# TensorE in program order, and transposes one slot later in three attentions

## The chip, the cores and the metric

The kernel runs on one core of a Trainium2 chip. A core has TensorE (PE: matmuls and transposes, into PSUM), VectorE (DVE), ScalarE (ACT), GpSimd (POOL) and SyncE (SP, whose queue issues the DMAs). Each engine works through its own list of instructions and waits where a semaphore says that an input or a buffer isn't there. The metric is the device time of one execution in microseconds, as the median of several runs.

## The reference, cut to what matters

Two transformer layers are computed one after the other in float32. The first, on 16 meta and 512 other tokens, has three branches on one projection: retention, differential attention (`probs0 - lam * probs1`, 8 heads) and a short convolution, then gates, an output product and a feed-forward part. The second, on 512 tokens and 256 context tokens, has a feed-forward part, projections, a neighbourhood attention (8 heads), a latent attention (8 heads, `softmax(q k^T) v`), gates and a second feed-forward part. Both layers use RMS norms:

```python
def rms_norm(x, w):
    xf = x.astype(jnp.float32)
    y = xf * lax.rsqrt(jnp.mean(xf * xf, axis=-1, keepdims=True) + EPS)
    return (y * w.astype(jnp.float32)).astype(x.dtype)
```

## The kernel before, in words

Every large product is computed with operands split in a high and a low part, three matmuls for one. Activations lie transposed in SBUF, features on partitions and tokens along the row. `Emitter._gemm` (its matmul is L231) takes 128 output columns at a time. For each it loops over the k tiles, and for each k tile over the three matmuls, into a PSUM buffer: `psg` or `pss`, two of each. Weights come by DMA as `raw`; ScalarE makes the high part `whi` (L132), VectorE or GpSimd the low part `wlo` (L136), in units of 512 columns with four buffers of each (`nhl=4`). The buffers of a unit come free when its matmuls have run.

The attentions are generators ("background"). While products are emitted, `tick` adds the model time of each matmul, `w / 2.4 + 3` ns, to a credit. Whenever it reaches the pace (3000 ns in retention, 900 in the differential, 750 in the neighbourhood and 700 in the latent attention), the generator is run to its next `yield`. At a `drain` it is run to its end. Each of the three attentions has 32 steps (head and block of 128 queries) in stages: `s0` scores on TensorE and the row maximum, `s1` the exponential and the scaling, `s2` transposes of the probabilities into PSUM (`pst`, two buffers) and their split into high and low parts, `s3` the product with v, and in the differential attention `s4` and `s5`, the norm and the transposes of its result. In slot t stage k handles step t - k, so a step's transposes come two slots behind its scores. The neighbourhood attention has at each head a matmul with `J` (L1511) that makes the bias table `TB`.

Norms run as a chain: sums of squares, a matmul with ones (`sums`, L330), some twenty tiny VectorE instructions, diagonal matrices, and a matmul (`spread`, L349) that lays the factor over all partitions. `em.after` puts the sums and the spread later in the emission by a given model time. `start2` emits the whole first chain at once, ahead of the first product.

What sets the order on the engines: the program is written out in full and then ordered by a scheduler. It plays the program through with a model of the durations. On each engine it picks, among the instructions that it takes as ready, the one of highest priority, which is the one emitted first (the weight splits are moved 30 places forward). So an instruction that isn't ready in the model is passed by others that were emitted after it. The lists so made are fixed when the kernel runs.

The names and lines of the steps: L231 weight products; L277 to L279 `mm3`, the scores in retention (h = q parts `qh`, `ql`) and in the latent attention (`mQ`, `mK`); L330 and L349 `sums` and `spread`; L806 transposes of the differential attention, whose input is `de`; `dvs`, that stage's split of the transposed v.

Of the kernel before, what the change touches and what calls it, by code (L numbers as in the profile page):

```python
# [6 lines left out]
F32 = mybir.dt.float32  # L7
F32R = mybir.dt.float32r
# [36 lines left out]
class Emitter:  # L45
# [19 lines left out]

    def open_streams(s, const, psum, nraw=3, nhl=4):
        s.sp, s.psum, s.nraw, s.nhl = const, psum, nraw, nhl


    def gemm(s, unit, cols, rhs, segs, evac, kt=KT):  # L70
# [140 lines left out]
    def _gemm(s, it):  # L211
        nc = s.nc
        jobs = it.segs if it.kind == "gemm" else it.chunks
        src = it.rhs if it.kind == "gemm" else it.lhs
        step = 512 // it.cols
        for si, job in enumerate(jobs):
            c0, w = job
            xh, xl = src(si)
            tag = s.rot[s.rot_i % len(s.rot)]
            s.rot_i += 1  # L220
            ps = s.psum.tile([128, 512 if tag == "g" else 1024], F32, name="ps" + tag, tag=tag, bufs=2)
            out = ps[0:it.cols, 0:w] if it.kind == "gemm" else ps[0:w, 0:it.cols]
            for k in range(it.kt):
                j = it.first + k // step
                s._step(j)
                cs = slice(it.cols * (k % step), it.cols * (k % step + 1))
                wh, wl = (t[:, cs] for t in s.hl[j])
                for m, (a, b) in enumerate(((wh, xh), (wh, xl), (wl, xh))):
                    b = b[:, k, c0:c0 + w]
                    l, r = (a, b) if it.kind == "gemm" else (b, a)  # L230
                    nc.tensor.matmul(out, l, r, start=(k == 0 and m == 0), stop=(k == it.kt - 1 and m == 2))  # L231
                    s._step()
                    s.tick(max(w if it.kind == "gemm" else it.cols, 64) / 2.4 + 3)
                if si == len(jobs) - 1 and (k == it.kt - 1 or k % step == step - 1):
                    s.hl.pop(j)
                    s._plan_split()
            s.late.append(lambda si=si, out=out: it.evac(si, out))
            s.flush_late(s.lag)


class Pools:
# [16 lines left out]

def emit(tc, d, out, dbg=None, stop=None):
    nc = tc.nc  # L260
    V, A, G, T, SP = nc.vector, nc.scalar, nc.gpsimd, nc.tensor, nc.sync
    pools = Pools(tc)
    em = Emitter(tc)
    psum = pools.open("psum", space=PSUM)
# [416 lines left out]
    DF = {}  # L681

    def d_evac(h, what):
        def f(si, ps):
            p, R1 = S["dp"], S["R1"]
            segs = TAIL if what == "q" else HALF
            c0, n = segs[si]
            r = R1[:, c0:c0 + n]
            A_, B_ = slice(0, 64), slice(64, 128)
            em.require(lambda: h < 2 or ("dS", h - 2) in GEMMED)  # L690
            if what == "q":
                v = p.tile([128, 512], F32, name="dev", tag="dev", bufs=2)
                DF[h, "q"] = [p.tile([128, 512], F32R, name=f"q{m}", tag=f"q{m}", bufs=2) for m in range(2)]
                hi = p.tile([128, 528], F32R, name="dhi", tag="dhi")
                lo = p.tile([128, 528], F32R, name="dlo", tag="dlo")
                V.tensor_mul(v, ps, r)
                act(hi[:, 0:512], v)
                sub_lo(G, lo[:, 0:512], v, hi[:, 0:512])
                for m, X in enumerate((A_, B_)):
                    spill(DF[h, "q"][m][A_], hi[X, 0:512])  # L700
                    spill(DF[h, "q"][m][B_], lo[X, 0:512])
            elif what == "k":
                if si == 0:
                    DF[h, "k"] = [[p.tile([128, 528], F32R, name=f"k{e}{m}", tag=f"k{e}{m}", bufs=2) for e in "hl"]
                                  for m in range(2)]
                    DF["k"] = [p.tile([128, 528], F32R, name="d" + e, tag="d" + e) for e in ("hi", "lo")]
                hi, lo = DF["k"]
                v = p.tile([128, 512], F32, name="dev", tag="dev", bufs=2)
                V.tensor_mul(v[:, 0:n], ps, r)
                cs = slice(c0, c0 + n)  # L710
                act(hi[:, cs], v[:, 0:n])
                sub_lo(G, lo[:, cs], v[:, 0:n], hi[:, cs])
                if si == 1:
                    for m, X in enumerate((A_, B_)):
                        for k, src in zip(DF[h, "k"][m], (hi, lo)):
                            for Y in (A_, B_):
                                spill(k[Y], src[X])
            else:
                if si == 0:
                    DF[h, "v"] = p.tile([128, 528], F32, name="dvt", tag="dvt", bufs=2)  # L720
                V.tensor_mul(DF[h, "v"][:, c0:c0 + n], ps, r)
            if si == len(segs) - 1:
                GEMMED.add(("d", h, what))
        return f
# [3 lines left out]
    def diff_bg():  # L728
# [3 lines left out]
        def s0(i):  # L732
# [3 lines left out]
                t = L["T", h] = p.tile([128, 528], F32, name="dT", tag="dT")  # L736
                V.tensor_scalar_mul(t, S["dbase"], -8.0 * 2.0 ** (-(h + 1)))
            tb = L["T", h]
            e = L["e", i] = p.tile([128, 2, 528], F32, name="de", tag="de", bufs=3)
            sm = L["sm", i] = p.tile([128, 8], F32, name="dsm", tag="dsm", bufs=3)  # L740
            ps, src = None, []
            for m in range(2):
# [109 lines left out]
            hilo(S["dfh"][:, h, :], S["dfl"][:, h, :], ps, w08)  # L852

        stages = (s0, s1, s2, s3, s4, s5)
        order = (5, 4, 1, 3, 0, 2)
        stage_runs = lambda k, i: k == 3 or i % 4 == 3
        for slot in range(32 + len(stages) - 1):
            if slot < 32:
                while ("d", slot // 4, "v") not in GEMMED:
                    yield False  # L860
            for k in order:
                if 0 <= slot - k < 32:
                    sub = stages[k](slot - k)
                    if sub is not None:
                        yield from sub
                    if k < 3 or stage_runs(k, slot - k):
                        yield

    em.low_parts(G, G)
# [601 lines left out]
    def stack(n, what, first, t0, u):  # L1471

        p = S["na"]
        N = 512 if what == "q" else 768
        cs = slice(t0, t0 + u.shape[-1])
        if first:
            NA["hl"] = [p.tile([128, 768], F32R, name="n" + c, tag="n" + c) for c in ("hi", "lo")]
        hi, lo = NA["hl"]
        act(hi[:, cs], u)
        sub_lo(G, lo[:, cs], u, hi[:, cs])  # L1480
        if t0:
            return
        if what == "q":
            NA[n, "q"] = [p.tile([128, 512], F32R, name=f"nq{e}", tag=f"nq{e}", bufs=2) for e in range(2)]
        else:
            NA[n, "k"] = [[p.tile([128, 768], F32R, name=f"nk{c}{e}", tag=f"nk{c}{e}", bufs=2) for c in "hl"]
                          for e in range(2)]
        for e, X in enumerate((A_, B_)):
            if what == "q":
                spill(NA[n, "q"][e][A_], hi[X, 0:N])  # L1490
                spill(NA[n, "q"][e][B_], lo[X, 0:N])
            else:
                for k, src in zip(NA[n, "k"][e], (hi, lo)):
                    for Y in (A_, B_):
                        spill(k[Y], src[X])
# [3 lines left out]
    def na_bg():  # L1499
# [3 lines left out]
        def s0(i):  # L1503
# [16 lines left out]
            wl = 128 * (hi - lo)  # L1520
            w = wl + 256
            q = NA[n, "q"][e][:, 128 * j:128 * j + 128]
            P_ = L["P", i] = p.tile([128, 640], F32, name="nP", tag="nP", bufs=3)
            sm = L["sm", i] = p.tile([128, 4], F32, name="nsm", tag="nsm", bufs=4)
            ps = pss()
            for a, c0, cw in ((512 - wl, 128 * lo, wl), (512, 512, 256)):
                for m, k in enumerate(NA[n, "k"][e]):
# [64 lines left out]
                GEMMED.add(("na", n))  # L1592

        stages = (s0, s1, s2, s3)
        order = (1, 3, 0, 2)
        stage_runs = lambda k, i: i % 4 == 3
        for slot in range(32 + len(stages) - 1):
            if slot < 32:
                while ("na", slot // 8, "v") not in GEMMED:
                    yield False  # L1600
                if slot % 8 == 0:
                    vprep(slot // 8)
            for k in order:
                if 0 <= slot - k < 32:
                    sub = stages[k](slot - k)
                    if sub is not None:
                        yield from sub
                    if k < 3 or stage_runs(k, slot - k):
                        yield

    def fold(o, p, e, oh, ol, w=512):
# [66 lines left out]
    def ml_bg():  # L1678
# [3 lines left out]
        def s0(i):  # L1682
# [4 lines left out]
                ml_load(h + 1)  # L1687
            Q, K = ML["Q", e], ML["K", e]
            qs = slice(128 * j, 128 * j + 128)
            P_ = L["P", i] = p.tile([128, 2, 384], F32, name="mP", tag="mP", bufs=3)  # L1690
            sm = L["sm", i] = p.tile([128, 4], F32, name="msm", tag="msm", bufs=4)
            ps = pss()
            L["S", i] = ps.rearrange("p (a k) -> p a k", a=2)[:, :, 0:384]
# [39 lines left out]
            fold(o, p, e, S["OMH"][:, n, q0:q0 + 256], S["OML"][:, n, q0:q0 + 256], 256)  # L1733

        stages = (s0, s1, s2, s3)
        order = (1, 3, 0, 2)
        stage_runs = lambda k, i: i % 2 == 1
        for slot in range(32 + len(stages) - 1):
            for k in order:
                if 0 <= slot - k < 32:  # L1740
                    sub = stages[k](slot - k)
                    if sub is not None:
                        yield from sub
                    if k < 3 or stage_runs(k, slot - k):
                        yield

    def ona_evac(n):
# [228 lines left out]
```

## Time and profile before

| what | value |
|---|---|
| median of three runs | 2831.26 us (2831.24 to 2832.66) |
| the profiled execution | 2835.28 us |
| its span, first to last instruction | 2833.3 us |
| mean granted TensorE clock | 0.984 |
| TensorE matmuls, weight loads | 97%, 85% of the span |
| VectorE, ScalarE, GpSimd | 57%, 39%, 30% |

The profiled execution is one execution; the rows and sums below are of its span, and the 2 us around it belong to its time. TensorE's ends are modelled, so a busy TensorE need not be at its peak.

### The profile page before, as it was taken

To read this page: it belongs to the slowest core of one execution; us is meant where nothing else is said; L and a number is where in the kernel's file an instruction comes from. 1 tells how busy PE (TensorE), PEld (TensorE's weight loads), DVE (VectorE), ACT (ScalarE), POOL (GpSimd) and SP (SyncE) were. 2 spreads that over 40 slices of the span, in tenths; PEclk is the share of its full clock that TensorE was granted. 3 is DMA by queue.
4 is the path that set the end of the run, shared out by engine and by line. 5 is a ranking of instruction groups with operands and counts; after the bars stand their busy time and mean duration, and the time that the engine had idled before them with its cause. 6 is when DMAs were issued, how large, how long until landed. Compare 5 with 4: busy or idle time off the path is not lost.

```text
span 2833.3 us, 42915 instructions
## 1 busy us (share of the span) xinstructions
PE 2736.0 (97%) x16308; PEld 2405.3 (85%) x16308; DVE 1620.0 (57%) x3318; ACT 1092.5 (39%) x2201; POOL 849.9 (30%) x710
## 2 busy tenths in 40 slices
PE   9999999999999889899999999979999999899997
PEld 8889988888878667788888888868889998899897
DVE  6554422377757999555223233496576876834346
ACT  4333322445534222243222122354455665633233
POOL 0223323433324233242111112442333224323224
PEclk9999999999999999999999999989999999999998
DMA  4222222443225658332121221334643424332324
GB/s 136 73 68 91 96 97 93 129 125 102 83 93 191 205 195 295 114 108 68 53 75 60 61 66 60 93 117 156 179 102 103 133 62 162 133 97 90 93 94 127
DMA packets 115998, 316.95 MB, mean 112 GB/s; under 512 B 21680, under 2 KB 35376, under 8 KB 115536
## 3 DMA queue, kind: packets, MB, share of 16 engines
q1 hardware_dynamic: 115792, 314.21, 35.5%
q8 instruction: 129, 2.11, 0.3%
q14 instruction: 77, 0.63, 0.1%
HBM read 279.09 MB, written 13.83 MB: 103 GB/s over the span
## 4 chain that ended last, share of the span: by engine, by line
PE 80%; DVE 14%; issue 3%; ACT 2%; DMA 0%; POOL 0%; POOLq 0%; DVEq 0%; SPq 0%; ACTq 0%
PE psg L231 49%; PE pss L231 22%; DVE wlo L136 2%; DVE wa L995 2%; DVE wx L995 1%; PE pss L277 1%; PE pst L827 1%; PE pss L278 1%; PE pss L279 1%; PE pst L1731 1%; PE pst L1717 1%; PE pss L1528 1%; PE pst L824 0%; DVE ut L1045 0%; DVE mg L1224 0%
## 5 line engine op out<-in xcount | busy, mean ns | idle before, releaser
L136 POOL TENSOR_TENSOR wlo<-raw,whi 128x512 fp32r<-128x512 f32 (+1 forms) x442 | 580.1, 1313 | 1568.4 <-ACT whi L132 1527.4
L132 ACT ACTIVATE whi<-raw 128x512 fp32r<-128x512 f32 (+1 forms) x844 | 522.7, 622 | 927.8 <-PE psg L231 588.8
L136 DVE TENSOR_TENSOR wlo<-raw,whi 128x512 fp32r<-128x512 f32 (+1 forms) x402 | 314.0, 782 | 452.6 <-ACT whi L132 451.9
L231 PE MATMUL psg<-xl,whi 128*128 128x264 f32 (+2 forms) x1104 | 362.7, 329 | 0.9 <-DVE xl L403 0.9
L231 PE MATMUL psg<-xh,whi 128*128 128x264 f32 (+2 forms) x1104 | 361.4, 328 | 1.7 <-ACT whi L132 1.2
L231 PE MATMUL psg<-xh,wlo 128*128 128x264 f32 (+2 forms) x1104 | 361.7, 328 | 0.0
L231 PE MATMUL psg<-XH,whi 128*128 128x256 f32 (+3 forms) x984 | 308.2, 313 | 1.8 <-DVE ft L1136 1.0
L231 PE MATMUL psg<-XH,wlo 128*128 128x256 f32 (+3 forms) x984 | 308.2, 313 | 0.0
L231 PE MATMUL psg<-XL,whi 128*128 128x256 f32 (+3 forms) x984 | 307.8, 313 | 0.0
L231 PEld LDWEIGHTS psg<-xh,whi 128*128 128x128 f32 x1104 | 209.0, 189 | 18.8 <-ACT whi L132 1.4
L231 PEld LDWEIGHTS psg<-xl,whi 128*128 128x128 f32 x1104 | 209.1, 189 | 18.5 <-DVE xl L403 1.5
L231 PEld LDWEIGHTS psg<-xh,wlo 128*128 128x128 f32 x1104 | 209.2, 190 | 17.0 <-DVE wlo L136 0.2
L231 PE MATMUL pss<-XL,whi 128*128 128x256 f32 (+2 forms) x600 | 191.3, 320 | 6.1 <-DVE XL L1208 6.1
L231 PEld LDWEIGHTS psg<-XH,whi 128*128 128x128 f32 (+1 forms) x984 | 185.4, 188 | 11.5 <-issue 2.4
L231 PEld LDWEIGHTS psg<-XH,wlo 128*128 128x128 f32 (+1 forms) x984 | 185.8, 189 | 10.5 <-issue 0.2
L231 PEld LDWEIGHTS psg<-XL,whi 128*128 128x128 f32 (+1 forms) x984 | 185.8, 189 | 9.3
L231 PE MATMUL pss<-XH,wlo 128*128 128x256 f32 (+2 forms) x600 | 191.4, 319 | 1.2 <-DVE wlo L136 1.2
L231 PE MATMUL pss<-XH,whi 128*128 128x256 f32 (+2 forms) x600 | 190.9, 319 | 0.5 <-DVE fs L1128 0.5
L231 PEld LDWEIGHTS pss<-XL,whi 128*128 128x128 f32 x600 | 114.9, 192 | 14.3 <-DVE XL L1208 7.3
L231 PEld LDWEIGHTS pss<-XH,wlo 128*128 128x128 f32 x600 | 115.4, 192 | 10.1 <-DVE wlo L136 1.6
L231 PEld LDWEIGHTS pss<-XH,whi 128*128 128x128 f32 x600 | 114.9, 192 | 7.5 <-DVE fs L1128 0.7
L231 PE MATMUL pss<-hh,wlo 128*128 128x256 f32 (+1 forms) x296 | 101.8, 344 | 7.5 <-DVE wlo L136 7.5
(558 smaller groups left out, 6444.6 us busy)
## 6 DMA issues: line engine op xcount, KB each, us to landing
raw<-w SPq DMA_DIRECT2D x142, 512.0 KB, 3.3
raw<-wi SPq DMA_DIRECT2D x96, 512.0 KB, 3.3
wa<-wa SPq DMA_DIRECT2D x72, 512.0 KB, 4.2
raw<-wq SPq DMA_DIRECT2D x38, 512.0 KB, 3.5
raw<-wu SPq DMA_DIRECT2D x32, 512.0 KB, 4.2
raw<-wd SPq DMA_DIRECT2D x32, 512.0 KB, 4.1
raw<-wb SPq DMA_DIRECT2D x24, 512.0 KB, 3.2
raw<-wo SPq DMA_DIRECT2D x24, 512.0 KB, 4.0
```

The source lines that it names most:

```text
L132: s.nc.scalar.activation(h, raw, AF.Copy)
L136: eng.tensor_sub(l, raw, h.bitcast(F32))
L231: nc.tensor.matmul(out, l, r, start=(k == 0 and m == 0), stop=(k == it.kt - 1 and m == 2))
L277: T.matmul(o, wh, xh, start=first, stop=False)
L278: T.matmul(o, wh, xl, start=False, stop=False)
L279: T.matmul(o, wl, xh, start=False, stop=last)
L827: T.matmul(o, x[:, c, :], vs[:, c, :], start=False, stop=c == b and m == 1)
L995: V.tensor_tensor_reduce(o, w, sb[:, s_, :], 1.0, 0.0, ALU.mult, ALU.add, S["modc"][:, s_, j:j + 1])
L1528: T.matmul(ps[:, a:a + cw], q, k[:, c0:c0 + cw], start=m == 0, stop=m == 1)
L1717: T.transpose(ps[:, 128 * c:128 * c + 128], P_[:, 128 * (c0 + c):128 * (c0 + c) + 128], ident)
L1731: T.matmul(o[:, 0:256], v[:, c, :], x[:, c, :], start=c == 0 and m == 0, stop=c == 5 and m == 1)
```

## The change

Every matmul and transpose is made through a wrapper, which ties it to the instruction that TensorE got before it. The scheduler may not move one past another any more; the other engines are ordered as before. In the three attentions stage `s2` and the stages behind it come one slot later, so the transposes stand three slots behind the scores. Tiles that live a slot longer get one buffer more (`de`, `nP`, `nsm`, `mP`), and the high and low parts of q and k that are copied by DMA get two buffers instead of one (`dhi`, `dlo`, `nhi`, `nlo`).

```diff
     def open_streams(s, const, psum, nraw=3, nhl=4):
         s.sp, s.psum, s.nraw, s.nhl = const, psum, nraw, nhl
+        s.pe = InOrder(s.tc, s.nc.tensor)
...
-                    nc.tensor.matmul(out, l, r, start=(k == 0 and m == 0), stop=(k == it.kt - 1 and m == 2))
+                    s.pe.matmul(out, l, r, start=(k == 0 and m == 0), stop=(k == it.kt - 1 and m == 2))
...
+class InOrder:
+
+
+    def __init__(s, tc, eng):
+        s.tc, s.eng = tc, eng
+
+    def matmul(s, *a, **kw):
+        s.tc.keep_in_program_order(s.eng.matmul(*a, **kw))
+
+    def transpose(s, *a, **kw):
+        s.tc.keep_in_program_order(s.eng.transpose(*a, **kw))
+
+
...
-    V, A, G, T, SP = nc.vector, nc.scalar, nc.gpsimd, nc.tensor, nc.sync
+    V, A, G, T, SP = nc.vector, nc.scalar, nc.gpsimd, InOrder(tc, nc.tensor), nc.sync
...
-                hi = p.tile([128, 528], F32R, name="dhi", tag="dhi")
-                lo = p.tile([128, 528], F32R, name="dlo", tag="dlo")
+                hi = p.tile([128, 528], F32R, name="dhi", tag="dhi", bufs=2)
+                lo = p.tile([128, 528], F32R, name="dlo", tag="dlo", bufs=2)
...
-            e = L["e", i] = p.tile([128, 2, 528], F32, name="de", tag="de", bufs=3)
+            e = L["e", i] = p.tile([128, 2, 528], F32, name="de", tag="de", bufs=4)
...
         stages = (s0, s1, s2, s3, s4, s5)
+        lags = (0, 1, 3, 4, 5, 6)
         order = (5, 4, 1, 3, 0, 2)
         stage_runs = lambda k, i: k == 3 or i % 4 == 3
-        for slot in range(32 + len(stages) - 1):
+        for slot in range(32 + lags[-1]):
...
             for k in order:
-                if 0 <= slot - k < 32:
-                    sub = stages[k](slot - k)
+                i = slot - lags[k]
+                if 0 <= i < 32:
+                    sub = stages[k](i)
                     if sub is not None:
                         yield from sub
-                    if k < 3 or stage_runs(k, slot - k):
+                    if k < 3 or stage_runs(k, i):
                         yield
...
-            NA["hl"] = [p.tile([128, 768], F32R, name="n" + c, tag="n" + c) for c in ("hi", "lo")]
+            NA["hl"] = [p.tile([128, 768], F32R, name="n" + c, tag="n" + c, bufs=2) for c in ("hi", "lo")]
...
-            P_ = L["P", i] = p.tile([128, 640], F32, name="nP", tag="nP", bufs=3)
-            sm = L["sm", i] = p.tile([128, 4], F32, name="nsm", tag="nsm", bufs=4)
+            P_ = L["P", i] = p.tile([128, 640], F32, name="nP", tag="nP", bufs=4)
+            sm = L["sm", i] = p.tile([128, 4], F32, name="nsm", tag="nsm", bufs=5)
...
-            P_ = L["P", i] = p.tile([128, 2, 384], F32, name="mP", tag="mP", bufs=3)
+            P_ = L["P", i] = p.tile([128, 2, 384], F32, name="mP", tag="mP", bufs=4)
```

The loops of the neighbourhood and the latent attention get `lags = (0, 1, 3, 4)` in the same way.

## Rows read from the trace of the kernel before

**Rows 1.** The page's engine table: busy us, share of the span, instructions.
```profile
PE 2736.0 (97%) x16308; PEld 2405.3 (85%) x16308; DVE 1620.0 (57%) x3318; ACT 1092.5 (39%) x2201; POOL 849.9 (30%) x710
```

**Rows 2.** Stretches: length, then busy us of each engine, granted clock, DMA share, GB/s.
```profile
530.00:792.00 262.00, 252.89 (x1604) 219.98 (x1603) 186.05 (x561) 133.75 (x376) 96.95 (x80) 0.99 0.37 107
...
1300.00:1400.00 100.00, 100.00 (x566) 87.24 (x565) 40.02 (x68) 28.04 (x49) 18.31 (x18) 1.00 0.19 59
...
2020.00:2330.00 310.00, 308.31 (x2159) 287.75 (x2158) 234.22 (x610) 177.41 (x398) 87.05 (x70) 1.00 0.41 106
```

**Rows 3.** TensorE's waits from 530 to 792: total us, times, longest.
```profile
PE pst L806 <- DVE dvs L274: 4.8, 4, 2.0
```

**Rows 4.** Timeline of the start (start, us), and L349 there.
```profile
7.89 0.39 PE L231 MATMUL psg<-xh,whi 128*128 128x264 f32 x1 [1.22 <-ACT whi L132]
...
19.03 0.69 DVE L136 TENSOR_TENSOR wlo<-raw,whi 128x512 fp32r<-128x512 f32 x1
...
19.27 1.08 PE L330 MATMUL pst<-ones,acc 128*128 128x1 f32 x10
...
L349 PE MATMUL pst<-acc,ones x4: 258/436/697, 25.9 to 27.1; 128*128 128x512 f32 x2, 16*128 16x16 f32 x2
```

**Rows 5.** Stretches of L231 alone: length, matmuls' and loads' busy us (count), clock, DMA.
```profile
7.89:25.90 18.01, 16.01 (x95) 13.27 (x95) 1.00 0.71 238
...
71.90:74.40 2.50, 2.12 (x17) 1.88 (x15) 1.00 0.00 0
...
87.70:88.90 1.20, 1.20 (x5) 0.81 (x5) 1.00 0.00 0
...
532.80:536.10 3.30, 3.21 (x13) 2.16 (x13) 1.00 0.90 206
...
786.80:790.70 3.90, 2.72 (x12) 1.87 (x10) 1.00 0.13 33
...
1290.60:1293.40 2.80, 2.80 (x13) 2.07 (x11) 1.00 0.01 3
...
1862.00:1882.80 20.80, 17.17 (x124) 16.16 (x124) 0.89 0.29 92
...
1953.60:1960.10 6.50, 6.25 (x30) 4.85 (x28) 1.00 0.81 295
...
2031.00:2043.00 12.00, 9.79 (x54) 7.76 (x52) 1.00 0.54 128
...
2170.00:2181.60 11.60, 9.42 (x74) 8.97 (x73) 1.00 0.67 171
...
2457.60:2463.60 6.00, 5.85 (x50) 5.64 (x48) 1.00 0.51 173
```

**Rows 6.** Timeline in retention, second head: VectorE's `ql` and the scores.
```profile
73.34 0.98 DVE L274 TENSOR_TENSOR ql<-ev,qh 128x512 fp32r<-128x512 f32 x1 [0.70 <-ACT qh L271]
...
74.39 0.50 PE L278 MATMUL pss<-ql,kh 128*128 128x512 f32 x1
```

**Rows 7.** A stretch of the neighbourhood attention, columns as in rows 2.
```profile
2040.00:2055.00 15.00, 15.00 (x96) 13.20 (x94) 13.34 (x38) 9.45 (x22) 5.71 (x5) 1.00 0.56 117
```

**Rows 8.** The latent attention: an issue, `mQ` from issue to landing, the first scores.
```profile
2176.19 0.58 SPq L1674 DMA_DIRECT2D mQ<-qr_d  x1
...
DMA to landing us min/median/max: 5.4/6.8/8.0
...
2189.86 0.34 PE L277 MATMUL pss<-mK,mQ 96*128 96x384 f32 x1
```

**Rows 9.** A wait of a transpose, and two stretches as in rows 2.
```profile
578.85 0.33 PE L806 MATMUL pst<-ident,de 128*128 128x128 f32 x1 [1.99 <-DVE dvs L274]
...
580.00:583.00 3.00, 3.00 (x16) 3.00 (x15) 2.75 (x12) 0.30 (x1) 0.00 (x0) 0.50 0.79 181
...
938.00:948.00 10.00, 5.08 (x12) 3.17 (x11) 9.83 (x15) 1.26 (x2) 2.55 (x2) 0.50 0.52 170
```

More of the change, by code (lines that the diff above doesn't have):

```diff
@@ L705, in f @@
                                   for m in range(2)]
-                    DF["k"] = [p.tile([128, 528], F32R, name="d" + e, tag="d" + e) for e in ("hi", "lo")]
+                    DF["k"] = [p.tile([128, 528], F32R, name="d" + e, tag="d" + e, bufs=2) for e in ("hi", "lo")]
                 hi, lo = DF["k"]
@@ L1594, in na_bg @@
         stages = (s0, s1, s2, s3)
+        lags = (0, 1, 3, 4)
         order = (1, 3, 0, 2)
         stage_runs = lambda k, i: i % 4 == 3
-        for slot in range(32 + len(stages) - 1):
+        for slot in range(32 + lags[-1]):
             if slot < 32:
@@ L1603, in na_bg @@
             for k in order:
-                if 0 <= slot - k < 32:
-                    sub = stages[k](slot - k)
+                i = slot - lags[k]
+                if 0 <= i < 32:
+                    sub = stages[k](i)
                     if sub is not None:
                         yield from sub
-                    if k < 3 or stage_runs(k, slot - k):
+                    if k < 3 or stage_runs(k, i):
                         yield
@@ L1735, in ml_bg @@
         stages = (s0, s1, s2, s3)
+        lags = (0, 1, 3, 4)
         order = (1, 3, 0, 2)
         stage_runs = lambda k, i: i % 2 == 1
-        for slot in range(32 + len(stages) - 1):
+        for slot in range(32 + lags[-1]):
             for k in order:
-                if 0 <= slot - k < 32:
-                    sub = stages[k](slot - k)
+                i = slot - lags[k]
+                if 0 <= i < 32:
+                    sub = stages[k](i)
                     if sub is not None:
                         yield from sub
-                    if k < 3 or stage_runs(k, slot - k):
+                    if k < 3 or stage_runs(k, i):
                         yield
```

## The prediction

> **What bounds the kernel now.** The page's engine table comes first: TensorE is busy 2736.0 us of the 2833.3 us span, 97%, and its weight loads 2405.3 us [rows 1]. All of TensorE's idle time together is therefore 97 us, and in a stretch such as 1300 to 1400 us there is none: 100.00 us busy at the full granted clock [rows 2]. Second, the waits: the largest group in the attentions is a transpose's, 4.8 us in four waits [rows 3]. So the change can give back little, and the question is what it takes away. Now the scheduler picks, among matmuls and transposes whose inputs it takes as ready, the one emitted first; one that isn't ready is passed by. Afterwards nothing is passed. I therefore followed the code's emission order and looked in the timeline for matmuls that run ahead of an instruction emitted before them. Each such place is a wait that is filled today. Its price is the busy time of the line that fills it, L231, from where TensorE would first stand before the waiting instruction to where that one's inputs are there [rows 5]. TensorE has no slack behind most of these places, so a filled wait that becomes an empty one moves the end.
>
> **The change part by part.**
>
> *Start.* `start2` emits the sums (L330) and the spread of R1 (L349) ahead of every weight product. In the rows the first weight product starts at 7.89 us, the sums at 19.27, the spread at 25.9 [rows 4]. Between, L231 ran 95 matmuls, 16.0 us [rows 5]. In program order none of them may run before the spread. The chain in front of it shortens a little: four weight splits run on VectorE between sums and spread, some 0.68 us each, the first at 19.03 [rows 4]. Their buffers come free only when products run, so they fall out of the chain: 2.7 us. Cost 16.0 - 2.7 = 13.3 us; bounds 10 and 16.
>
> *Retention.* The scores are emitted right behind the q product, whose evacuation is not done. The scores' second matmul runs at 74.39, when `ql` of 73.34 + 0.98 us is there [rows 6]; L231 filled 2.1 us. The transposes of v wait likewise for a PSUM buffer, 1.2 us [rows 5]. Each comes once for each of four heads: 4 x 2.1 + 4 x 1.2 = 13.2 us. Bounds 8 (if the evacuation comes sooner when it has VectorE alone) and 16.
>
> *Differential attention.* 3.2 us at the first scores, which wait for spilled q and k, and 2.7 us at the last transposes, which wait for the norm [rows 5]: 5.9 us. What of the idle time goes? The transposes L806 wait on `dvs` [rows 3], which is the evacuation that frees their PSUM buffer, not their input. That evacuation belongs to the same stage and moves along, so I credit the later slot with nothing here; bounds 0 and the whole 4.8 us.
>
> *Output product and the layer after it.* Two spreads, each like the one at 1290.6, which fills 2.8 us [rows 5], and the sums ahead of each, about half that (an estimate from it): 8.4 us; bounds 5 and 9.
>
> *Second projections (1828 to 1965 us).* Two updates hang in one chain on VectorE. From 1862 to 1882.8 L231 ran 124 matmuls, 17.2 us [rows 5]. The code emits 55 of them ahead of the second spread, so 69 are left undone: 17.2 x 69 / 124 = 9.6 us. Two spreads after it are alike, and the one at 1953.6 fills 6.25 us [rows 5]. Sum 9.6 + 2 x 6.25 = 22.1 us; bounds 12 (VectorE sets part of this stretch anyhow) and 30.
>
> *Neighbourhood attention.* While the bias matmul of an odd head and the transposes behind it wait, L231 ran 9.8 us from 2031 on [rows 5], the first of three such places. Here the later slot helps: three yields of 750 ns pace cover 2.25 us, which leaves at most 7.5 us in each. Nothing says that all of it stays, since TensorE then feeds VectorE less. Yet VectorE is busy 13.34 of 15 us in such a place [rows 7], and the PSUM buffers (two) that the transposes need are freed by it. I take 5 us in each and 3 us for the last heads, 18 us; bounds 0 and 30. More buffers for `nP` and `nhi` cost nothing, no queue holds them.
>
> The Trainium skill (Perfetto Trace Analysis, Identifying the Most-Contended Engine) says that a gap which keeps coming back can mean that buffers in SBUF or PSUM ran out. By that rule the added SBUF buffers would take these waits away only if SBUF were what is short. The waits in [rows 3] and [rows 7] point at PSUM, which the change leaves at two buffers, so the sum would stay by either.
>
> *Latent attention.* The first scores need q and k, whose loads are queued behind the last stage's end; q's last part is issued at 2176.19, and the soonest of these loads lands after 5.4 us, at 2181.6 [rows 8]. From 2170 to 2181.6 L231 filled 9.4 us [rows 5]. These scores are emitted after only a few products, so 9.4 us; bounds 6 and 17 (TensorE ran them only at 2189.86 [rows 8]). After its start the stage runs as emitted and has hardly an idle moment; later transposes give nothing.
>
> *The end (2397 to 2834 us).* The last spread of the update pair fills 5.85 us [rows 5], and I give the final one the 2.8 us of 1290.6. The second chain starts some 3 us later than now, since products emitted before its sums still have to run (an estimate, half of the last spread's fill). Sum 11.7 us; bounds 6 and 18.
>
> *Clock.* TensorE now falls to half, 1.2 GHz, after waits: after 1.99 us without work the stretch 580 to 583 us shows 0.50, and 938 to 948 us after a longer one [rows 9]. Ten busy microseconds at half lose 5, three lose 1.5. With some thirty new waits of 1 to 13 us I take 10 us in all; bounds 0 and 35.
>
> *Relief.* A waiting TensorE asks for no splits and evacuations, so the awaited chains come sooner: one tenth of the filled time, -10 us; bounds 0 and -45.
>
> The sum: 13.3 + 13.2 + 5.9 + 8.4 + 22.1 + 18 + 9.4 + 11.7 = 102.0 us, +10 - 10. The transposes' later slot adds one slot at the end of each attention; other products run there, cost nothing, a microsecond each if they were gone.
>
> **Rivals.**
>
> *The order of now is itself what costs.* If TensorE's waits came from the scheduler's picks, program order with later transposes would take the attentions' idle time away: 9.1 us in 530 to 792 and 1.7 us in 2020 to 2330 [rows 2], with the half clock that follows some 13 us, so 2822 us. It decides only if filled waits elsewhere cost less than 13 us, and the start alone costs that. For it speaks that the transposes' waits are the largest there; against it, that they wait for PSUM.
>
> *TensorE isn't the bound and absorbs the waits:* no change, 2831 us. For it speaks only that weight loads are at 85% [rows 1]; against it, the stretches with no idle time at all [rows 2].
>
> The Trainium skill (same page and section) counts weight-load share as the better measure of TensorE's headroom, not matmul busy time. By it 15% of the span, 428 us, would be free. This trace disagrees: in 1300 to 1400 us loads are busy 87.24 us while TensorE never idles [rows 2].
>
> *The chains come much sooner once TensorE waits* (a relief of half): about 2831 + 45 = 2876, down to 2850.
>
> *Waits breed waits:* late evacuations and half clock in every stage, all upper bounds: 2980 to 3030 us. It decides if the clock stays at half for much of retention and neighbourhood attention.
>
> *The order isn't kept* would leave 2831 us; every matmul goes through the new wrapper, so I give it nothing apart.
>
> **How the numbers follow.** The profiled execution took 2835.28 us (span 2833.3 and 2 around it); with 102 it is 2937 us. The median of the runs is 4 us lower, so 2933 us. Chances: this forecast (2880 to 2980) 0.70, chains much sooner 0.14, waits breed waits 0.09, no change 0.03, faster 0.04. The range 2865 to 2990 leaves out faster, no change, most of the breeding waits and some of the sooner chains. Within 0.2%, 5.7 us, a measurement can't tell from no change: faster 0.04, same 0.03, slower 0.93.
>
> **What would show it.** After: the first L231 matmul behind L349, at 23 to 26 us, with TensorE idle from 6.7 us but for the sums; L278 waiting some 2 us on `ql`, four times; L349 and L330 among the largest waits, on VectorE and ScalarE; the first latent scores right after their load, behind an idle stretch of 6 us or more; TensorE's busy total near 2736 us and its idle time near 190; a granted clock below 0.984. The forecast is wrong if products still run before L330 at the start, if the idle total stays near 97 us, or if L806's waits on `dvs` vanish and other stages don't grow. Then either the order isn't kept, or the chains are much shorter when nothing competes with them.

## The result, and the profile after

The changed kernel takes 2938.25 us in the median of four runs (2937.62 to 2940.23); the kernel before, in the same set, 2831.96 us. The ratio is 1.0376, 95% interval 1.0358 to 1.0394: 106 us slower, where 102 were forecast. The range (2865 to 2990) holds the time.

The engine table of the page after, which answers to [rows 1]:

```profile
PE 2759.4 (94%) x16308; PEld 2425.5 (83%) x16308; DVE 1618.1 (55%) x3318; ACT 1091.7 (37%) x2201; POOL 848.8 (29%) x710
```

The span is 2935.8 us. TensorE's idle time is the span less its busy time, 176.4 us, against 2833.3 - 2736.0 = 97.3 before. So 79.1 of the 102.5 us by which the span grew are idle time, and 23.4 us are the same 16308 matmuls taking longer. The second part goes with a lower granted clock; the cores' view, before and then after:

```profile
core 0: 2833.3 us, clock 0.984
```

```profile
core 0: 2935.8 us, clock 0.971
```

With two levels, 2.4 and 1.2 GHz, a mean of 0.984 is 2 x 0.016 x 2833.3 = 91 us at half, and 0.971 is 170 us. Summed over the stretches at half, TensorE is busy in 54 of the former and in 112 of the latter; the rest of that time it stands idle.

Where did it go? The same VectorE, ScalarE and GpSimd instruction (line, tiles, count) can be found in both traces. The median shift of those around a stage's bound says how late the changed kernel is there, and gives the bounds after that answer to those before. Stretches of the kernel after, with the columns of [rows 2]:

```profile
0.00:61.40 61.40, 41.28 (x243) 36.71 (x244) 32.95 (x82) 24.61 (x46) 2.24 (x6) 0.81 0.39 132
61.40:280.30 218.90, 209.82 (x1322) 185.86 (x1321) 110.80 (x236) 64.99 (x112) 46.28 (x37) 0.98 0.21 68
560.30:836.40 276.10, 262.97 (x1660) 228.44 (x1659) 188.25 (x568) 137.64 (x382) 100.25 (x82) 0.99 0.37 105
836.40:1338.80 502.40, 466.25 (x1969) 371.93 (x1968) 370.99 (x550) 159.15 (x274) 175.59 (x121) 0.96 0.51 168
1338.80:1861.60 522.80, 522.80 (x2911) 453.75 (x2911) 173.55 (x291) 143.28 (x245) 105.59 (x95) 1.00 0.21 65
1861.60:2024.90 163.30, 127.29 (x841) 115.95 (x841) 120.46 (x278) 73.00 (x166) 55.77 (x51) 0.87 0.32 102
2074.90:2245.60 170.70, 156.36 (x998) 140.41 (x997) 115.41 (x319) 80.12 (x185) 45.08 (x38) 0.95 0.39 98
2245.60:2487.70 242.10, 232.45 (x1624) 220.51 (x1623) 161.77 (x356) 132.40 (x286) 67.13 (x54) 0.98 0.39 112
2487.70:2571.10 83.40, 64.75 (x465) 61.53 (x465) 67.17 (x150) 47.62 (x105) 30.37 (x33) 0.92 0.35 118
2891.10:2935.80 44.70, 27.55 (x212) 25.64 (x211) 31.40 (x72) 12.67 (x27) 15.89 (x19) 0.85 0.34 108
```

A row's idle time is its length less the first number behind it; the column "before" of the table is made in the same way from the trace of before. "Slower matmuls" is what the stage grew less what its idle time grew. It is negative in the differential attention, which has two half-clock spells before and one after.

| stage (bounds before) | longer | idle before, after | slower matmuls | forecast |
|---|---|---|---|---|
| start, 0 to 45 | 16.4 | 4.2, 20.1 | 0.5 | 13.3 |
| retention, 45 to 250 | 13.9 | 0.7, 9.1 | 5.5 | 13.2 |
| differential attention, 530 to 805 | 1.1 | 9.1, 13.1 | -2.9 | 5.9 |
| output product and the layer after, 805 to 1820 | 10.2 | 30.5, 36.1 | 4.6 | 8.4 |
| second projections, 1820 to 1965 | 18.3 | 20.5, 36.0 | 2.8 | 22.1 |
| neighbourhood attention, 2015 to 2165 | 20.7 | 1.0, 14.3 | 7.4 | 18 |
| latent attention, 2165 to 2395 | 12.1 | 2.1, 9.7 | 4.5 | 9.4 |
| the end, 2395 to 2833 | 9.8 | 27.1, 35.9 | 1.0 | 11.7 |

The sum of the second column is 102.5 us. Nothing is lost between 250 and 530, where TensorE doesn't stand still in either trace, and each stage that lost has idle time in it that was not there.

Who waits for what, in TensorE's waits over the whole kernel after (us, times, longest):

```profile
PE pst L249 <- DVE accy L1226: 21.5, 4, 9.5
PE psg L249 <- ACT uh L285: 16.6, 6, 4.7
PE pst L249 <- ACT RF L285: 16.2, 8, 4.4
PE pst L249 <- DVE acc L428: 13.1, 1, 13.1
...
PE pst L252 <- DVE nvt L1480: 8.2, 4, 2.1
PE pst L252 <- DVE dvs L288: 7.6, 8, 2.1
PE pss L249 <- ACT qh L285: 5.3, 4, 1.3
```

All matmuls now have the wrapper's line, L249, and all transposes L252; the tile says which is meant. `acc` and `accy` are the sums of a norm, `RF` the spread, `qh` the scores of retention, `nvt` the v of the neighbourhood attention, which the transposes read. The waits on `uh` and `dvs` were there before too. The PSUM buffer and the inputs tell who waits. Over the whole listing, the waits of products come to 62.1 us before and 49.8 after; those of sums, spreads, scores, transposes and the attentions' products to 22.7 and 114.8.

The start, in TensorE's timeline after, which answers to [rows 4]:

```profile
5.28 0.50 PE L249 MATMUL pst<-ones 128*128 128x128 f32 x3
18.91 2.01 PE L249 MATMUL pst<-ones,acc 128*128 128x1 f32 x10 [13.13 <-DVE acc L428]
24.33 2.04 PE L249 MATMUL pst<-acc,ones 128*128 128x512 f32 x2 [3.41 <-DVE acc L354]
```

Between 5.78 and 24.33 us TensorE does the sums and nothing else, and the first product starts at 26.84. Before, 95 products ran from 7.89 to 25.9 [rows 5].

Retention after, at the first head (the second of [rows 6] is like it), in the timeline of ScalarE and TensorE:

```profile
39.91 0.63 ACT L285 ACTIVATE qh<-ev 128x512 fp32r<-128x512 f32 x1 [0.26 <-DVE ev L481]
...
40.59 0.50 PE L249 MATMUL pss<-qh,kh 128*128 128x512 f32 x1 [1.32 <-ACT qh L285]
```

The latent attention's first scores after, which answer to [rows 8]:

```profile
2261.06 2.26 PE L249 MATMUL pss<-mK,mQ 96*128 96x384 f32 x6 [3.46 <-DMA mQ<-qr_d]
```

They now start as soon as the load is there, behind an idle stretch, and not 8 us later. The load was issued at 2254.42, so it took 6.6 us.

### The profile page after: what moved, and what is told of

It reads as the page before. It is cut to its first block, busy times and chain, and to the rows that moved or that the text cites. A ratio compares the mean times of both kernels' runs of the same rounds, so it can differ in the third digit from the quotient of the medians.

```text
span 2935.8 us, 42893 instructions
## 1 busy us (share of the span) xinstructions
PE 2759.4 (94%) x16308; PEld 2425.5 (83%) x16308; DVE 1618.1 (55%) x3318; ACT 1091.7 (37%) x2201; POOL 848.8 (29%) x710
## 4 chain that ended last, share of the span: by engine, by line
PE 54%; DVE 10%; issue 2%; ACT 1%; DMA 0%; POOL 0%; SPq 0%; POOLq 0%; DVEq 0%; ACTq 0%
PE psg L249 28%; PE pss L249 23%; PE pst L249 3%; DVE wlo L137 2%; PE pst L252 1%; DVE wa L1011 1%; DVE wx L1011 1%; DVE mg L1240 0%; DVE XL L1224 0%; DVE ut L1062 0%; DVE ut L1061 0%; DVE ul L288 0%; ACT whi L133 0%; DVE xx L1240 0%; DVE ga L1777 0%
## 5 line engine op out<-in xcount | busy, mean ns | idle before, releaser
L249 PE MATMUL psg<-xl,whi 128*128 128x264 f32 (+2 forms) x1104 | 362.9, 329 | 0.0
L249 PE MATMUL psg<-xh,wlo 128*128 128x264 f32 (+2 forms) x1104 | 361.6, 328 | 0.0
L249 PE MATMUL psg<-xh,whi 128*128 128x264 f32 (+2 forms) x1104 | 361.6, 328 | 0.0
L249 PE MATMUL psg<-XH,wlo 128*128 128x256 f32 (+3 forms) x984 | 310.4, 315 | 1.1 <-DVE wlo L137 1.1
L249 PE MATMUL psg<-XH,whi 128*128 128x256 f32 (+3 forms) x984 | 309.6, 315 | 0.0
L249 PE MATMUL psg<-XL,whi 128*128 128x256 f32 (+3 forms) x984 | 309.4, 314 | 0.0
L249 PEld LDWEIGHTS psg<-xl,whi 128*128 128x128 f32 x1104 | 209.5, 190 | 17.2
L249 PEld LDWEIGHTS psg<-xh,whi 128*128 128x128 f32 x1104 | 209.6, 190 | 17.1
L249 PEld LDWEIGHTS psg<-xh,wlo 128*128 128x128 f32 x1104 | 209.8, 190 | 16.0
L249 PEld LDWEIGHTS psg<-XH,wlo 128*128 128x128 f32 (+1 forms) x984 | 187.9, 191 | 12.9 <-DVE wlo L137 1.6
L249 PEld LDWEIGHTS psg<-XH,whi 128*128 128x128 f32 (+1 forms) x984 | 188.1, 191 | 9.8 <-issue 0.2
L249 PEld LDWEIGHTS psg<-XL,whi 128*128 128x128 f32 (+1 forms) x984 | 188.2, 191 | 9.4
L249 PE MATMUL pss<-XH,whi 128*128 128x256 f32 (+2 forms) x600 | 191.2, 319 | 1.5 <-DVE fs L1144 1.4
L249 PE MATMUL pss<-XH,wlo 128*128 128x256 f32 (+2 forms) x600 | 192.2, 320 | 0.2 <-DVE wlo L137 0.2
L249 PE MATMUL pss<-XL,whi 128*128 128x256 f32 (+2 forms) x600 | 191.6, 319 | 0.0
L249 PEld LDWEIGHTS pss<-XH,wlo 128*128 128x128 f32 x600 | 115.9, 193 | 8.1 <-DVE wlo L137 0.4
L249 PEld LDWEIGHTS pss<-XH,whi 128*128 128x128 f32 x600 | 115.3, 192 | 8.6 <-ACT whi L133 1.6
L249 PEld LDWEIGHTS pss<-XL,whi 128*128 128x128 f32 x600 | 115.6, 193 | 7.1 <-DVE XL L1224 0.2
L249 PE MATMUL pss<-hh,wlo 128*128 128x256 f32 (+1 forms) x296 | 101.3, 342 | 5.7 <-DVE wlo L137 5.5
```

Source lines behind the costliest of these rows:

```text
L249: s.tc.keep_in_program_order(s.eng.matmul(*a, **kw))
```

## The experiments

The theory: the loss is products that ran while an earlier-emitted instruction waited, and that may not pass it any more; the later slot and the buffers are worth next to nothing. The rivals: the later slot does something of its own (for or against), or any fixed order costs. All times are medians; each ratio is to the kernel before, run in the same set, where its median was 2831.83 to 2833.03 us. TensorE's idle time is that of the one profiled execution.

| kernel | median us | ratio, 95% interval | TensorE idle us |
|---|---|---|---|
| changed kernel | 2938.25 | 1.0376 [1.0358, 1.0394] | 176.4 |
| later slot and buffers, no order | 2831.03 | 0.9992 [0.9983, 1.0001] | 98.9 |
| buffers alone, no order | 2835.03 | 1.0008 [0.9999, 1.0017] | 97.4 |
| later slot in the differential attention alone, no order | 2831.31 | 0.9993 [0.9984, 1.0002] | 96.2 |
| order alone | 2943.13 | 1.0393 [1.0377, 1.0409] | 178.4 |
| two rows: products, and all the rest | 2841.18 | 1.0033 [1.0020, 1.0045] | 103.5 |
| norms outside the order | 2892.74 | 1.0212 [1.0198, 1.0226] | 137.6 |
| order, old slots in the last two attentions | 2934.30 | 1.0356 [1.0342, 1.0370] | 176.6 |
| the same once more | 2934.12 | 1.0361 [1.0344, 1.0378] | 175.4 |
| order, start and retention arranged by hand | 2921.57 | 1.0311 [1.0297, 1.0325] | 159.1 |
| order, transposes of v three paces later | 2929.33 | 1.0342 [1.0327, 1.0357] | 169.6 |

**The later slot without the order.**

```diff
     def matmul(s, *a, **kw):
-        s.tc.keep_in_program_order(s.eng.matmul(*a, **kw))
+        s.eng.matmul(*a, **kw)
```

(and the same for `transpose`)

> Only the later slot and the added buffers; the scheduler orders TensorE as before. Theory (the filled waits cost, the later slot does nothing, because the transposes wait for PSUM): 2826 to 2838 us, within 0.2% of before, and the waits of the transposes on dvs stay near 4.8 us. Rival (the transposes' place is what costs, and the later slot takes that away): about 2822 us, with the dvs waits gone. Rival (the longer pipeline itself costs, so part of the 106 us is its own): 2845 us or more.

It takes 2831.03 us, the same time as before. The waits on `dvs` stay, 4.9 us in six (before 4.8 in four, [rows 3]). The theory holds; both rivals fall.

**The order without the later slot:** the kernel before with the wrapper, slots and buffers as they were.

> Only the program order on TensorE; slots and buffers as before. Theory: the whole loss comes from here, and the later slot gives back up to 3 x 2.25 us in the neighbourhood attention, so 2938 to 2946 us. Rival (the later slot helps much once the order is kept): 2955 us or more. Rival (the later slot is part of the loss): 2925 us or less.

It takes 2943.13 us: the whole loss comes from the order. By the medians the later slot and its buffers then give 5 us back, as was expected, though the two intervals overlap; the place is another. The differential attention of this kernel:

```profile
558.50:842.90 284.40, 268.93 (x1660) 232.02 (x1659) 193.34 (x568) 137.86 (x382) 100.22 (x83) 0.98 0.36 102
```

It is 9.4 us longer than before, where that of the changed kernel is 1.1 longer (and that of the five other kernels with the order, or most of it, and the later slot in it 1.2 to 2.8). In the two later attentions it is the other way about: the order alone loses 25.2 us from 2015 to 2395, the changed kernel 32.8.

**Two rows instead of one:**

```diff
-        s.tc.keep_in_program_order(s.eng.matmul(*a, **kw))
+        s._behind_last(s.eng.matmul(*a, **kw))
```

where `_behind_last` ties an instruction to the last one that was made by the same wrapper. The products have one wrapper, sums, spreads, scores, transposes and the rest another.

> As the changed kernel, but TensorE's work is tied in two separate rows: the weight products behind one another, and all the rest behind one another; the scheduler may interleave the two. Theory (the loss comes from products that may not pass a waiting sum, spread, score or transpose): nearly all of the 106 us comes back, 2831 to 2850 us, idle time of TensorE near 100 us. Rival (the order inside one of the rows costs, for instance a product that may not pass a product): 2880 us or more.

It takes 2841.18 us. Of the 106 us 97 are back though every product still runs behind the one emitted before it, and every transpose too. The sums at the start, in TensorE's timeline, run without a wait and with products before and behind them:

```profile
19.57 0.40 PE L257 MATMUL pss<-xh,wlo 128*128 128x512 f32 x1
19.80 1.08 PE L257 MATMUL pst<-ones,acc 128*128 128x1 f32 x10
20.82 0.51 PE L257 MATMUL pss<-xh,whi 128*128 128x512 f32 x1
```

So it isn't order as such that costs; it is that a product may not pass what waits for another engine. The 9 us that are left are clear of no change. At the second projections the products' own waits on `XL`, their input's low part, come to 7.7 us where they were 3.3, so the rival (a product that may not pass a product) seems to hold there on a small scale.

**The norms outside the order:** `sums` and `spread` go past the wrapper, all else stays in one row.

> As the changed kernel, but the sums and spreads of the norms are left out of the tied row, so the scheduler may place them. Theory: the start, the layer after the output product, the second projections and the end come back, which by the drift between the traces of before and after are 16.4 + 7.4 + 2.9 + 18.2 + 8.4 + 1.4 = 54.7 us, so about 2884 us (2875 to 2895); retention, neighbourhood and latent attention stay as in the changed kernel. Rival (one delay only hides the next, so freeing one kind shifts the wait to another): 2910 us or more.

It takes 2892.74 us, 45.5 less than the changed kernel; the theory said 54.7. By stages the layer after the output product and the end are back to 1.4 us below and 0.4 us above before, the second projections to 4.2, retention and neighbourhood attention stay (13.8 and 19.1). The start misses: it stays 9.1 longer. Half of that is idle time, mostly its scores, which now wait 3.6 us for `qh`; the other half is slower matmuls, at a granted clock of 0.84. Thus part of the rival is true there: one freed delay leaves the next standing.

**The later slot in the differential attention alone, and the buffers alone,** both with the scheduler's order.

> TensorE ordered by the scheduler as before; the later slot and its buffers in the differential attention alone. In the kernel with the later slot everywhere that attention came out 4.8 us shorter, and the two others gave 1 to 3 us back. Theory (the later slot is worth something there and there alone): 4 to 5 us faster than before, ratio 0.9983. Rival (the 4.8 us were a chance of one profile): no difference, ratio 1.0000.

> All added buffers, nothing in another slot, TensorE ordered by the scheduler as before. Theory (the buffers alone do nothing): the same time as before, within 0.1%. Rival (the second buffer of the high and low parts is what shortened the differential attention): 4 to 5 us faster, ratio 0.9983.

Neither differs from before by more than the 0.2% that can be told from no change. In its profile the first comes out 3.8 us shorter in that attention, like the 4.8 of the kernel with all later slots. But the times don't confirm it, and the theory of this pair fell: the profiled execution of before is 4 us above its own median, with a half-clock spell in this very stage [rows 9]. The Trainium skill (Perfetto Trace Analysis, Optimization Strategy, where the prediction names the section ahead of it) says that a bubble that repeats can come from too little SBUF or PSUM; the buffers-only run shows that here it isn't the SBUF buffers that were added.

**The old slots in the last two attentions, with the order.**

```diff
-        lags = (0, 1, 3, 4)
+        lags = (0, 1, 2, 3)
```

> The changed kernel, its program order too, with the neighbourhood and the latent attention back in their old slots; the buffers stay. By the stages of the order-only kernel against the changed one, the later slot costs 7.6 us there. Theory: about 2931 us. Rival (the later slot covers part of the waits, as the prediction had it): 2945 us. Rival (neutral): 2938 us.

It takes 2934.30 us, and 2934.12 the second time. For that second run this was expected:

> The changed kernel with the neighbourhood and the latent attention in their old slots, once more, beside the run with v's transposes moved, so that the later slot's cost there has a second measurement: 2934 us if the 4 us of the first stand, 2938 us if they were chance.

Both say 4 us less than the changed kernel. By the medians that is the cost of the later slot there, though the two intervals still overlap with the changed kernel's; by the stages, 2015 to 2395, it is 7.5 in the one profile and 4.3 in the other: without the later slot 25.3 and 28.5 us are lost there, with it 32.8 (and 32.6 in the kernel arranged by hand, below). Single executions differ nearly as much (the first was taken in an execution 2.8 us below its median, that of the order alone 3.9 below), so a cost of about 4 us there is likely, not certain; the 2945 us of the rival by which the later slot covers part of the waits are ruled out.

**Two places arranged by hand, within the order.**

```diff
-            rnorm(S["R1"], acc, D, acc2)
+            em.after(11000, lambda: rnorm(S["R1"], acc, D, acc2, gap=2250))
...
             while ("r", h, "q") not in GEMMED:
                 yield False
+            yield
```

`depth(DEEP, 3)` goes with it (the first evacuations lag three products behind), the norm's two tiles live in another pool, and the transposes of v get the same `yield`.

> The changed kernel, its program order too, with the fill of two places written into the program: the first norm's sums come after 11.0 us of products and its spread 2.25 us later, the first evacuations lag three products behind, and in retention the scores and the transposes of v come one pace later. Theory (not the order costs, but what stands in it behind a wait): the start and retention come back, 16 + 14 us less some 3 us that the spread still waits, so 2908 to 2916 us, TensorE's idle time near 153 us. Rival (a fixed order costs wherever the time on the chip differs from the program's guess): 2925 us or more.

It takes 2921.57 us, 16.7 less than the changed kernel: between the theory's bounds and the rival's. The idle time came back at the start (6.0 us there, 20.1 in the changed kernel) and the waits on `qh` are gone; retention's four waits on `vl` are not:

```profile
PE pst L252 <- DVE vl L288: 4.1, 4, 1.2
PE pst L252 <- DVE y L576: 2.9, 3, 1.5
```

They stand between the pieces of one step (three groups of transposes in a row, two PSUM buffers), so it doesn't help to move the step. And the start stays 7.5 us longer with only 1.8 us more idle time. Of the other 5.7 some 2 are matmuls that moved in (262 in that stretch, 250 before; an estimate from their mean, 0.16 us); the rest goes with the clock. Two stretches of this kernel:

```profile
7.00:10.00 3.00, 1.35 (x7) 0.93 (x7) 2.77 (x5) 3.00 (x7) 0.00 (x0) 1.00 1.03 388
10.00:17.00 7.00, 5.91 (x23) 5.09 (x24) 7.00 (x12) 7.00 (x13) 0.00 (x0) 0.51 0.82 283
```

**The transposes of v later, within the order.** The trace of the changed kernel names the wait that costs most in the neighbourhood attention. VectorE and TensorE there:

```profile
2079.65 1.35 DVE L1480 TENSOR_SCALAR nvt<-nvt,bt 128x512 f32<-128x512 f32 x1
```

```profile
2081.06 0.88 PE L252 MATMUL pst<-ident,nvt 128*128 128x128 f32 x6 [2.05 <-DVE nvt L1480]
```

The transposes stand right behind v's product, and v's evacuation isn't done. The edit is three `yield` lines ahead of them.

> The changed kernel with one place of the neighbourhood attention written in another position: the transposes of v come three paces (2.25 us) after v's last evacuation instead of right behind it, four times. In the changed kernel these four waits on nvt are 8.2 us, and half-clock spells of 3.4 us, worth 1.7 us each, begin behind them. Theory (position and clock): 8 us of idle time and up to 6.8 us of half clock come back, so 2922 to 2931 us. Rival (the wait moves to the scores and the matmul with J behind it, which the later transposes hold up): 2935 us or more. Rival (only the idle time, the clock falls anyway): 2930 us.

It takes 2929.33 us, 8.9 less. The waits on `nvt` are gone. From 2060 to 2300 us this kernel's TensorE waits are led by

```profile
PE pst L252 <- DVE npxl L288: 5.7, 5, 1.6
PE pst L249 <- DVE nv L288: 3.2, 4, 1.2
PE pst L249 <- DVE npxl L288: 2.2, 3, 0.8
```

In the changed kernel those on `npxl` are 5.2 us and those on `nv` 1.4. So 4.5 us of waiting came back behind the place. The idle time of the whole kernel fell by 6.8 us, but TensorE's busy time by 0.8 only, as if the half clock had cost as much as before. The two attentions behind the edit, in the changed kernel and then in this one, say otherwise:

```profile
2074.90:2487.70 412.80, 388.81 (x2619) 360.92 (x2618) 277.18 (x674) 212.52 (x470) 112.21 (x92) 0.97 0.39 106
```

```profile
2077.60:2479.90 402.30, 384.55 (x2619) 356.71 (x2618) 278.36 (x675) 212.78 (x470) 112.73 (x92) 0.98 0.39 109
```

They are 10.5 us shorter: 6.2 of idle time, and 4.3 by which the same 2619 matmuls take less. What hides this in the sum is that the start, retention and the differential attention, which the edit leaves alone, have 4.0 us more busy time in this one execution. So the theory (position and clock) fits the place, while the time alone lies in its range and a hair from the last rival's 2930 us.

## Why the prediction was right

**The mechanism.** All of it is the order (order alone 1.0393, later slot alone 0.9992), and it is products held up by waiting instructions (two rows 1.0033). The Trainium skill (PSUM — Partial Sum Buffer, Engine vs sequencer instructions) says that matmuls start and complete in program order; the trace agrees, since nothing at all runs in the 13.13 us ahead of the sums. Only what is listed ahead of an instruction can fill its wait, and the prices could be read from what had filled it. The waits say the same: the products' own fell from 62.1 to 49.8 us, all others grew from 22.7 to 114.8, by 92 us where 102 had been priced.

**The start, retention, output product, second projections, the end.** Forecast 13.3, 13.2, 8.4, 22.1 and 11.7, measured 16.4, 13.9, 10.2, 18.3 and 9.8. The agreement is partly luck: the prices are of idle time alone, and the lengths hold slower matmuls too. Idle time grew by 15.9, 8.4, 5.6, 15.5 and 8.8 us; of the start's, 2.5 are the waits of retention's first head (`qh` 1.3, `vl` 1.0, `ql` 0.2), so the start itself gave 13.4 and retention 10.9. Only the start reached its price. In retention the scores waited 7.1 us in all where 8.4 were priced, mostly on `qh` and not on `ql` as forecast, and v's transposes 3.9 where 4.8 were. The chain at the start came 1.6 us sooner (spread at 24.33 instead of 25.9), not 2.7. Hand arrangement and norms outside the order show these causes; what the second spread of the second projections alone costs was only read from the trace.

**The differential attention.** 5.9 forecast, 1.1 measured. The sentence that failed credits the later slot with nothing here. With the scheduler's order that is what it is worth; with the fixed order it gives some 7 to 8 us by the stages. The times agree: the order alone takes 1.0393 [1.0377, 1.0409], and with the later slot in this attention alone and all buffers 1.0356 [1.0342, 1.0370] and, the second time, 1.0361 [1.0344, 1.0378]; no run parts the slot from the buffers there. Of the 8.3 us between the order alone and the changed kernel, 2.3 are idle time and 6.0 the same 1660 matmuls taking less (268.93 and 262.97 us). Why is open: the waits on `dvs` even grow (5.4 to 7.6 us), other waits shrink.

**The neighbourhood attention.** 18 forecast, 20.7 measured, but not for the reason given. I let the matmul with `J` and the transposes wait for PSUM and the later slot cover 2.25 us of each. The largest wait is v's transposes on v's own evacuation, and the later slot doesn't move them; where it acts it seems to cost some 4 us. Idle time grew by 13.3 us, and 7.4 are slower matmuls. The errors went against each other.

**The latent attention.** 9.4 forecast, 12.1 measured up to 2395. The wait on the load is 3.46 us, where an idle stretch of 6 or more was to be the sign; the load took 6.6 us, where the sum took the soonest of four, 5.4. The rest is shorter waits and 4.5 us of slower matmuls.

**Clock and relief.** 10 us were forecast for half clock; TensorE's busy time grew by 23.4. Relief was to be 10; idle time grew by 79.1 where 102 were filled, so it was 23. Some 12 of these are the products' own waits, which the forecast didn't name, and 10 are waits that came out shorter than what had filled them. Both terms are mis-sized, by 13 each, and cancel: the sum was right by luck in this part. The Trainium skill (TensorE: Matmul & The Clock Gate, HAM oscillation — how this bites in real kernels) reckons the penalty as half the throttled time. For the 79 us more at half that would be 40 us, an estimate by that page; this case shows 23.4. Part of the time at half is time in which TensorE waits: it was busy in 54 of 90 us before and in 112 of 170 after.

**The rivals.** That the present order costs, and that TensorE absorbs the waits, both fall. That chains come much sooner is true in part: the relief is 23 of 102, not half.

## What to carry to other kernels

Before an order is fixed, look for what now runs ahead of an instruction emitted earlier: each such place is a wait in the fixed order, and what fills it is its price. Where an order is wanted, tie like to like (products behind products), and leave free the relation of the two kinds, or emit each consumer of a chain as late as the chain takes (two places by hand gave 17 us of 106 back, one more 9). And a gain of 4 us in one profile's stage is worth nothing until times confirm it.

## What the runs showed of the hardware

Two starts that look alike can get different clocks. Before, TensorE stood 1.22 us ahead of its first product [rows 4], and the stretch from 8 to 30 us ran at 1.00:

```profile
8.00:30.00 22.00, 20.31 (x124) 16.89 (x125) 18.83 (x59) 13.67 (x28) 0.00 (x0) 1.00 0.61 209
```

In the kernel arranged by hand it stood 1.28 us there, and the stretch from 10 to 17 us ran at 0.51 (shown above):

```profile
8.23 0.39 PE L249 MATMUL psg<-xh,whi 128*128 128x264 f32 x1 [1.28 <-ACT whi L133]
```

The first waits are alike, but what follows is not. From 8 to 10 us, before and then by hand:

```profile
8.00:10.00 2.00, 2.00 (x14) 1.71 (x14) 2.00 (x4) 2.00 (x4) 0.00 (x0) 1.00 1.03 373
```

```profile
8.00:10.00 2.00, 1.35 (x7) 0.93 (x7) 1.79 (x3) 2.00 (x5) 0.00 (x0) 1.00 1.04 370
```

By hand TensorE waited again, 0.22 and 0.20 us, before the clock fell. The kernel with two rows did nearly the same (1.17, 0.22 and 0.20 us) and also ran at half from 9.8 to 16.6 us. So a first short wait alone doesn't tell the clock behind it, and its half-clock cost, some microseconds, can't be forecast from these traces. Whether the further waits decide, or something that changes from one execution to the next, no run shows.
